# Seven half-width products for the queries of five heads, and an earlier first product for the gates, in a two-layer decoder on one Trainium2 core

## The chip, the cores and the metric

The kernel runs on one core of a Trainium2 chip, as one launch. The metric is the device time of that launch in microseconds; the median of several executions counts. Before the change it is 971.77 us (three runs, 971.26 to 971.91). One further execution was recorded by the hardware profiler.

## What is computed

A decoder trunk of two layers over 528 positions (16 learned meta tokens and 512 tokens) of width 1024, all in float32. The first layer is gated linear attention, the second differential attention with 8 heads. The change is in the second. Cut to it, the reference says:

```python
proj = xn @ w_in                                  # 528x1024 @ 1024x8192
q, k, v, z = jnp.split(proj, 4, axis=-1)          # each 8 heads x 256
s = q_m @ k_m.T * 128 ** -0.5 + bias              # two score maps a head, m = 0, 1
p = softmax(where(dist >= 0, s, -inf))
a = p[0] - lam * p[1]
o = head_rms(a @ v) * gnorm * (1 - lambda_init)
h = h + (silu(z) * o) @ w_out
```

Then a final RMSNorm is applied and the meta positions are dropped.

## The kernel before, in words

**Numbers in two parts.** Matrix products run on TensorE in a float32 form of less precision. Each operand x is therefore split: ScalarE writes a rounded part `hi`, VectorE the rest `lo = x - hi` (`split`, L270 to L280), and a product is three: hi hi, hi lo, lo hi. A weight tile of 128 x 1024 so costs one operation of 1024 elements on each of the two engines before it can be used. In the profile the parts are named wh and wl, a11h and a11l, q (both), k (both) and so on.

**Two ways to project.** The plain way (`project`, L414 to L425) makes a block of 128 outputs for 512 tokens from 8 pieces of the inner dimension, three products each: 24 matmuls of 512 columns a block; a head's 256 outputs are two blocks, 48 matmuls. The other way (`Unit`, L436 to L536) cuts weights and inputs in 2 x 2 blocks and makes the product from seven products of half size in place of eight (Winograd's form of Strassen's scheme), each of 12 matmuls over 256 columns (264 with the meta tokens): 84 matmuls. For it VectorE first forms sums of weight blocks (`want_unit`, L356 to L385: four additions of 512 elements), and weights are split as a11, a12 and a22 (512 elements each) and two pairs of sums (1024 each). The inputs' sums are made once for all heads. The products p1 to p7 go into PSUM banks bx, by and bv; ScalarE copies what the bank bx holds after p1, p6 and p7 (`partial`, L450, three copies u1, u2, u3 of a sum that grows), and VectorE adds the pieces (`add`, L472). The first product of a unit, p1 (`first`, L455), can be issued by the unit before it, so that its copy is done in time; such a unit is called early. A unit looks up what follows it in the queue when it starts (`following`, L86).

**The order of work.** TensorE's instructions stand in the order in which the code issues them. A `Weaver` (L74) holds a queue of generators, each a projection that yields its estimated time as it goes; `fill(us)` runs the head of the queue for so many estimated us. Between the steps of a head's attention the main loop (L1849 to L1905) calls `fill`, so that projections for the next head stand between the attention steps of this one: A is `scores` (L1679), B `turn` (L1703), C `values` (L1716), E `rows` (L1735), for four blocks of 128 queries each. The order in a steady head is: output projection of two earlier heads (`q_diff_out2`, L1766, half of the columns a head), gates z, values v, keys k, queries q for the next head. z, v and k are units of seven products; q is plain (`q_diff_q`, L1662). In head 6 the order is keys, queries, values, gates. The first `fill` of a head, 3.0 us, stands ahead of its first scores (L1888).

The instructions of the other engines are ordered by a scheduler with priorities; `soon`, `urgent` and `at_once` (L254 to L265) raise them by 40, 100 and 160. Each engine takes its instructions in that order, so one that waits holds up those behind it.

**Weights.** `Weights` (L154) loads 1 MB a unit through SP's queue into one of two buffers `raw`, and makes the split parts when a buffer of their kind is free: two of the pairs, one each of sum, a11, a12, a22. `done` (L199) gives a part's buffer back when its product has been issued. The values of a head are also turned by DMA: they leave through ScalarE's queue, and come back by transposes on SP's queue (L598, L600), which stand there ahead of the gates' weights.

**Scores.** For each block and each of the two maps, TensorE fills a bank ps, VectorE adds the bias T and takes the extreme (L1692), ScalarE takes the exponential and its sum (L1694). Then VectorE forms lam times the ratio of the two sums (L1697, L1698) and combines the maps (L1699).

Of the kernel before, what the change touches and what calls it, by code (L numbers as in the profile page):

```python
# [73 lines left out]
class Weaver:  # L74


    def __init__(self):
        self.queue, self.late, self.left, self.stop = deque(), [], 0.0, None
        self.away, self.behind, self.gated = [], [], ()
# [130 lines left out]
def trunk(ctx, tc, x, meta, g_norm, gla_w_in, gla_w_gate_up, gla_b_gate, gla_gnorm, gla_w_out,  # L210
# [53 lines left out]
    def at_once(fn):  # L264
        return urgent(fn, 160)  # L265
# [170 lines left out]
    class Unit:  # L436
# [17 lines left out]

        def first(self):  # L455
            a11 = self.u[0]
            w = ws.use(a11)
            self.bx = pb_tile(self.tags[0])
            yield from product(self.bx, w, self.X["b11"])
            ws.done(a11)  # L460
            self.p1 = self.partial()

        def run(self):
# [40 lines left out]
            def p7():  # L504
                yield from product(self.bx, ws.use(s43)[1], X["t3"], False)
                self.u3 = self.partial()
                add(1, 1, self.bv, self.u3, -1)
# [994 lines left out]
    up[0] = ep  # L1502
# [159 lines left out]
    def q_diff_q(hd, s):  # L1662
        want_diff(256 * hd)

        def gen():
            for i in range(2):
                bank = pb_tile("bx" if hd else ("bv", "by")[i])
                yield from project(ws.take(), real2, None, NR, [by_halves(bank)])
                assert not hd or heads[hd - 1].scored
                if i == 0:  # L1670
                    s.q = [T(ep, [P, 2, NR], F32R, f"q{j}", bufs=1) for j in range(2)]
                urgent(split)(*[t[:, i, :] for t in s.q], bank, scale=-float(P) ** -0.5)
        return W.add(gen(), 10.3)

    def diff_steps(hd, s, ys):
# [3 lines left out]
        def scores(b):  # L1679
# [4 lines left out]
            r.p = []  # L1684
            ko = L - nk
            for m in range(2):
# [8 lines left out]
                r.p.append(p[:, :nk])  # L1695
# [70 lines left out]
    def q_diff_out2(hd, yp, halves):  # L1766
# [5 lines left out]
        def gen():  # L1772
            for i in halves:
                banks = [pb_tile(tag) for tag in ("bx", "by", "bv", "bx")]
                cs = slice(512 * i, 512 * (i + 1))
                for j, h in enumerate(parts[i]):
                    w = ws.use(h)
                    for b in range(4):
                        for k in range(2):
                            y = [t[:, k, b * P:(b + 1) * P] for t in yp[j]]  # L1780
                            mm3(banks[b], y, w[k], j == k == 0, j == k == 1)
                        if j:
                            W.mark = dve.tensor_tensor(hacc[:, b, cs], hacc[:, b, cs], banks[b], op=ALU.add)
                        yield 1.4
                    ws.done(h)
# [62 lines left out]
    for hd in range(D_HEADS):  # L1848
# [39 lines left out]
        W.fill(3.0)  # L1888
# [80 lines left out]
```

## Time and profile before

| what | value |
|---|---|
| median of three runs | 971.77 us |
| the profiled execution's own time | 970.65 us |
| its span, first to last instruction | 968.9 us |
| TensorE busy (matmul) | 957.2 us, 99% |
| VectorE busy | 778.6 us, 80% |
| ScalarE busy | 626.8 us, 65% |
| GpSimd busy | 44.9 us, 5% |
| moved by DMA | 104.94 MB, mean 108 GB/s |

The page gives one execution. PE is TensorE's matmuls, PEld its weight loads, which overlap the matmuls; DVE is VectorE, ACT ScalarE, POOL GpSimd, SP the queue that issues loads. A row names the line, the engine, the operation, what it writes and reads (out<-in), the shape and the count; behind the bar stand busy time and mean ns, and then the idle time of the engine just before these instructions, with what ended it. Matmuls are pipelined, so that their durations overlap: the distance from one start to the next is what counts. A row in the slices gives, for a stretch of time, the busy time of PE, PEld, DVE, ACT and POOL with the number of instructions, then the granted clock of TensorE, the share in which the DMA engines were busy, and GB/s. A steady head of the second layer lasts some 63 us.

### The profile page before, as it was taken

To read this page: it belongs to the slowest core of one execution; us is meant where nothing else is said; L and a number is where in the kernel's file an instruction comes from. 1 tells how busy PE (TensorE), PEld (TensorE's weight loads), DVE (VectorE), ACT (ScalarE), POOL (GpSimd) and SP (SyncE) were. 2 spreads that over 40 slices of the span, in tenths; PEclk is the share of its full clock that TensorE was granted. 3 is DMA by queue.
4 is the path that set the end of the run, shared out by engine and by line. 5 is a ranking of instruction groups with operands and counts; after the bars stand their busy time and mean duration, and the time that the engine had idled before them with its cause. 6 is when DMAs were issued, how large, how long until landed. Compare 5 with 4: busy or idle time off the path is not lost.

```text
span 968.9 us, 18048 instructions
## 1 busy us (share of the span) xinstructions
PE 957.2 (99%) x6993; PEld 906.9 (94%) x6993; DVE 778.6 (80%) x1586; ACT 626.8 (65%) x1304; POOL 44.9 (5%) x68
## 2 busy tenths in 40 slices
PE   9999999999999999999999999999999999999997
PEld 8999999999999999998899998998999989989996
DVE  7989885886888787668997987968869769687785
ACT  7776755577647567656757776575675756755583
POOL 1000000000000000000001001000000000000001
PEclk9999999999999999999999999999999999999999
DMA  7322223635363236124355525243342341722212
GB/s 197 88 85 59 82 79 122 147 103 128 116 162 91 85 117 158 53 101 152 99 130 138 143 73 133 75 139 98 99 138 88 118 119 44 182 70 84 89 64 87
DMA packets 128522, 104.94 MB, mean 108 GB/s; under 512 B 51102, under 2 KB 112830, under 8 KB 128433
## 3 DMA queue, kind: packets, MB, share of 16 engines
q1 hardware_dynamic: 123104, 93.80, 35.1%
q10 hardware_dynamic: 5328, 9.95, 2.8%
q8 instruction: 56, 0.92, 0.4%
q14 instruction: 34, 0.27, 0.1%
HBM read 83.64 MB, written 11.80 MB: 99 GB/s over the span
## 4 chain that ended last, share of the span: by engine, by line
PE 88%; ACT 1%; DVE 1%; issue 1%; POOLq 0%; DVEq 0%
PE bx L431 19%; PE bv L431 12%; PE by L431 10%; PE bx L421 10%; PE ps L400 9%; PE bx L972 5%; PE bx L400 3%; PE bv L972 2%; PE by L972 2%; PE ps L1214 2%; PE by L400 2%; PE bv L400 2%; PE ps L1807 1%; PE bx L1807 1%; PE bv L421 1%; PE by L421 1%
## 5 line engine op out<-in xcount | busy, mean ns | idle before, releaser
L277 DVE TENSOR_TENSOR wl<-raw,wh 128x1024 fp32r<-128x1024 f32 x98 | 119.4, 1221 | 23.0 <-ACT wh L276 18.9
L276 ACT ACTIVATE wh<-raw 128x1024 fp32r<-128x1024 f32 x98 | 103.1, 1054 | 48.3 <-PE by L972 22.9
L431 PE MATMUL bv<-x,wh 128*128 128x264 f32 (+1 forms) x656 | 98.6, 287 | 0.0
L431 PE MATMUL bx<-x,wh 128*128 128x264 f32 (+1 forms) x640 | 95.6, 286 | 0.0
L431 PEld LDWEIGHTS bv<-x,wh 128*128 128x128 f32 x656 | 86.8, 189 | 0.6 <-DVE z L479 0.2
L431 PEld LDWEIGHTS bx<-x,wh 128*128 128x128 f32 x640 | 84.6, 188 | 0.7 <-ACT u L452 0.2
L452 ACT ACTIVATE u<-bx 128x264 f32<-128x264 f32 (+1 forms) x120 | 45.3, 379 | 35.5 <-PE bx L431 33.1
L1694 ACT ACTIVATE p<-p,st 128x528 f32<-128x528 f32 (+3 forms) x64 | 36.5, 570 | 41.7 <-DVE st L1692 41.4
L421 PE MATMUL bx<-x,wh 128*128 128x512 f32 (+1 forms) x256 | 62.4, 385 | 0.0
L277 DVE TENSOR_TENSOR wl<-sum,wh 128x1024 fp32r<-128x1024 f32 x41 | 50.1, 1221 | 10.6 <-ACT wh L276 10.5
L431 PE MATMUL bx<-x,wl 128*128 128x264 f32 (+1 forms) x320 | 54.1, 284 | 0.0
L431 PE MATMUL bv<-x,wl 128*128 128x264 f32 (+1 forms) x328 | 53.8, 284 | 0.1
L421 PEld LDWEIGHTS bx<-x,wh 128*128 128x128 f32 x256 | 44.4, 188 | 7.8
L276 ACT ACTIVATE wh<-sum 128x1024 fp32r<-128x1024 f32 x41 | 43.1, 1051 | 9.7 <-PE by L972 3.9
L431 PE MATMUL by<-x,a12h 128*128 128x264 f32 (+1 forms) x320 | 47.5, 286 | 0.1
L1730 POOL TENSOR_TENSOR st<-st,mhalf 128x1 f32<-128x1 f32 x32 | 25.5, 795 | 468.6 <-ACT on L1728 418.2
L431 PE MATMUL bx<-x,a11h 128*128 128x264 f32 (+1 forms) x320 | 46.6, 284 | 0.0
L431 PEld LDWEIGHTS bv<-x,wl 128*128 128x128 f32 x328 | 45.4, 188 | 0.3 <-issue 0.3
L431 PEld LDWEIGHTS bx<-x,wl 128*128 128x128 f32 x320 | 45.3, 188 | 0.3
L431 PEld LDWEIGHTS bx<-x,a11h 128*128 128x128 f32 x320 | 42.4, 188 | 0.6
L431 PEld LDWEIGHTS by<-x,a12h 128*128 128x128 f32 x320 | 42.1, 188 | 0.3 <-ACT t L1658 0.3
L276 ACT ACTIVATE a11h<-raw 128x512 fp32r<-128x512 f32 x41 | 25.7, 626 | 20.7 <-DMA raw<-in_diff_w_in_dram 7.9
(493 smaller groups left out, 2631.9 us busy)
## 6 DMA issues: line engine op xcount, KB each, us to landing
raw<-in_gla_w_in_dram SPq DMA_DIRECT2D x48, 512.0 KB, 4.5
raw<-in_diff_w_in_dram SPq DMA_DIRECT2D x42, 512.0 KB, 4.9
raw<-in_diff_w_in_dram SPq DMA_DIRECT2D x11, 1024.0 KB, 5.9
raw<-in_gla_w_out_dram SPq DMA_DIRECT2D x8, 1024.0 KB, 5.8
raw<-in_diff_w_out_dram SPq DMA_DIRECT2D x8, 1024.0 KB, 6.0
vd<-planes ACTq DMA_DIRECT2D x12, 268.0 KB, 5.8
vd<-keep ACTq DMA_DIRECT2D x12, 264.0 KB, 2.3
T<-bdr SPq DMA_DIRECT2D x8, 264.0 KB, 4.7
```

What stands on the lines that cost most here:

```text
L276: act.activation(hi, src, AF.Copy)
L277: dve.tensor_tensor(lo, src, hi.bitcast(F32), op=ALU.subtract)
L400: pe.matmul(ps, l, r, start=first and n == 0, stop=last and n == 2, **kw)
L421: pe.matmul(bank, a[:, k, :], b[k] if n0 is None else b[k][:, n0 + i * nn:n0 + (i + 1) * nn], start=n == 0 and ks[0] == 0, stop=n == len(t ...
L431: pe.matmul(bank[:, :x[q].shape[2]], w[p][:, k * P:(k + 1) * P], x[q][:, k, :], start=first and i == 0, stop=i == len(PASSES) - 1, skip_gr ...
L452: W.moved = act.activation(t, self.bx[:, :self.n], AF.Copy, scale=self.sc)
L972: pe.matmul(banks[i][:, :HT], h.t[p][:, k, mm * P:(mm + 1) * P], s.y[q][k][:, i * HT:(i + 1) * HT], start=n == 0, stop=n == len(PASSES) - 1)
L1214: pe.matmul(o, s.kd[:, i, kc], s.qs[:, i, t0:t0 + n], start=i == 0, stop=i == 1)
L1694: act.activation(p[:, :nk], p[:, :nk], AF.Exp, scale=-1.0, bias=st[:, m:m + 1], accum_out=st[:, 2 + m:3 + m])
L1730: pool.tensor_tensor(ms, ms, mhalf[:, :1], op=ALU.pow)
L1807: pe.matmul(ps[i], yp[hd][p][:, k, b * P:(b + 1) * P], wt[q][cs.start // 512][:, 2 * hd + k, cs.start % 512:(cs.stop - 1) % 512 + 1], star ...
```

## The change

The queries of heads 3 to 7 become units of seven products, with the scale in their additions and a split of the finished queries from SBUF. In the second layer a unit that is early and has no unit behind it, as these queries and the keys of heads 1 and 2 are, puts p7 into a bank of its own; VectorE adds it to u2 (`third`), in place of the growing sum in bx and ScalarE's copy. The output projection issues the first product of the gates behind it, ahead of the last of its own four groups; its additions to the residual get the highest priority. Of the two score maps, map 1 comes first. The first fill of a head is 4.0 us in place of 3.0.

```diff
@@ Weaver.__init__
-        self.away, self.behind, self.gated = [], [], ()
+        self.away, self.behind, self.gated, self.second = [], [], (), False
@@ class Unit
+        @at_once
+        def third(self, bank):
+            t = T(up[0], [P, HT], F32, "u", bufs=3)[:, :self.n]
+            if self.sc == 1.0:
+                dve.tensor_tensor(t, bank[:, :self.n], self.u2, op=ALU.add)
+            else:
+                dve.scalar_tensor_tensor(t, bank[:, :self.n], self.sc, self.u2, op0=ALU.mult, op1=ALU.add)
+            return t
+
@@ Unit.run
             def p7():
-                yield from product(self.bx, ws.use(s43)[1], X["t3"], False)
-                self.u3 = self.partial()
+                if W.second and early and not nxt:
+                    bank = pb_tile("bx")
+                    yield from product(bank, ws.use(s43)[1], X["t3"])
+                    self.u3 = self.third(bank)
+                else:
+                    yield from product(self.bx, ws.use(s43)[1], X["t3"], False)
+                    self.u3 = self.partial()
                 add(1, 1, self.bv, self.u3, -1)
@@ start of the second layer
-    up[0] = ep
+    up[0], W.second = ep, True
@@ q_diff_q
+        scale, qts = -float(P) ** -0.5, []
+
+        def tiles():
+            assert not hd or heads[hd - 1].scored
+            s.q = [T(ep, [P, 2, NR], F32R, f"q{j}", bufs=1) for j in range(2)]
+
+        if hd in (3, 4, 5, 6, 7):
+            def dst():
+                tiles()
+                qts.extend([tok_tile()[:, :NR], tok_tile()[:, :NR]])
+                return qts
+
+            @soon
+            def tail(i):
+                split(*[t[:, i, :] for t in s.q], qts[i])
+
+            return W.add(Unit(want_unit(d_w_in, 256 * hd), Xr, scale, dst, tail), 8.9)
         want_diff(256 * hd)
...
@@ scores
-            r.p = []
+            r.p = [None, None]
             ko = L - nk
-            for m in range(2):
+            for m in (1, 0):
...
-                r.p.append(p[:, :nk])
+                r.p[m] = p[:, :nk]
@@ q_diff_out2
         def gen():
+            nxt = W.following()
+            nxt = nxt if isinstance(nxt, Unit) else None
             for i in halves:
...
                         if j:
-                            W.mark = dve.tensor_tensor(hacc[:, b, cs], hacc[:, b, cs], banks[b], op=ALU.add)
+                            W.mark = at_once(dve.tensor_tensor)(hacc[:, b, cs], hacc[:, b, cs], banks[b], op=ALU.add)
                         yield 1.4
+                        if (i, j, b) == (halves[-1], 1, 2) and nxt:
+                            yield from nxt.first()
@@ main loop
-        W.fill(3.0)
+        W.fill(4.0)
```

On TensorE, at the end of head 4's queries (made during head 3) and the start of the output projection that head 4 issues, this stood before (bx is the second block of the plain query projection, then the output projection's first bank; ps the first scores, read from q and k):

```order
L421 MATMUL bx_11924<-x_1512_8554,wl_11870 128x512 x4
L421 MATMUL bx_11924<-x_1514_8556,wl_11870 128x512 x4
L400 MATMUL bx_11958<-wh_11971,y_1540_8780 128x512
L400 MATMUL bx_11958<-wl_11972,y_1540_8780 128x512
L400 MATMUL bx_11958<-wh_11971,y_1540_8780 128x512 x2
L400 MATMUL bx_11958<-wl_11972,y_1540_8780 128x512
L400 MATMUL bx_11958<-wh_11971,y_1540_8780 128x512
L400 MATMUL by_11959<-wh_11971,y_1540_8780 128x512
```

and this stands there now (by and bx take the products of a12 and a22, bv the last one; then again the output projection):

```order
L431 MATMUL by_12053<-x_1514_8556,a12l_11893 128x256 x4
L431 MATMUL bx_12067<-x_1544_8787,a22h_11990 128x256 x8
L431 MATMUL bx_12067<-x_1544_8787,a22l_11991 128x256 x4
L431 MATMUL bv_12013<-x_1514_8556,wh_11986 128x256
L431 MATMUL bv_12013<-x_1515_8557,wh_11986 128x256
...
L431 MATMUL bv_12013<-x_1514_8556,wl_11987 128x256 x4
L400 MATMUL bx_12098<-wh_12111,y_1540_8780 128x512
L400 MATMUL bx_12098<-wl_12112,y_1540_8780 128x512
```

The queries' 512-column products became products of 256 columns, and the output projection's groups follow at once as before, three of them ahead of the first scores in both.

On VectorE, at the same place, this stood before (a11l, sum, a12l and raw belong to head 5's gates, wl to the output projection, q to head 4's queries):

```order
L277 TENSOR_TENSOR a11l_11983<-raw_11968,a11h_11982 128x512
L277 TENSOR_TENSOR wl_11972<-raw_11962,wh_11971 128x1024
L280 SCALAR_TENSOR_TENSOR q_2134_11921<-bx_11878,q_2133_11920 128x512
L1740 TENSOR_TENSOR yt_11931<-ps_11928,z_10728 128x256
L366 TENSOR_TENSOR sum_11986<-raw_11968 128x512
...
L277 TENSOR_TENSOR a12l_12056<-raw_11968,a12h_12055 128x512
L366 TENSOR_TENSOR raw_11968<-raw_11968,sum_11986 128x4x128
L277 TENSOR_TENSOR wl_11976<-raw_11962,wh_11975 128x1024
L280 SCALAR_TENSOR_TENSOR q_2134_11921<-bx_11924,q_2133_11920 128x512
```

and now (u at L461 is the new third, t the additions of the queries' pieces):

```order
L461 SCALAR_TENSOR_TENSOR u_12046<-bx_12026,u_12011 128x256
...
L277 TENSOR_TENSOR a11l_12123<-raw_12108,a11h_12122 128x512
L490 SCALAR_TENSOR_TENSOR t_12050<-by_12053,u_11936 128x256
...
L486 SCALAR_TENSOR_TENSOR t_12051<-bx_12067,u_12046 128x256
L366 TENSOR_TENSOR sum_12126<-sum_12126,raw_12108 128x512
L366 TENSOR_TENSOR raw_12108<-raw_12108 128x4x128
L490 SCALAR_TENSOR_TENSOR t_12050<-bv_12013,u_12011 128x256
L277 TENSOR_TENSOR q_2165_12049<-t_12051,q_2164_12048 128x512
L277 TENSOR_TENSOR wl_12116<-raw_12102,wh_12115 128x1024
L277 TENSOR_TENSOR q_2165_12049<-t_12050,q_2164_12048 128x512
```

Four additions of the queries' pieces now stand among the work on the gates' weights, three of them behind a11l, and the query splits read their result from SBUF in place of PSUM.

5 lines of the change are left out of this document (2 added, 3 removed).

## The prediction

> **What bounds the kernel now.** I read the page first: span, busy shares, the chain that ended last.
>
> ```profile
> span 968.9 us, 18048 instructions
> PE 957.2 (99%) x6993; PEld 906.9 (94%) x6993; DVE 778.6 (80%) x1586; ACT 626.8 (65%) x1304; POOL 44.9 (5%) x68
> PE 88%; ACT 1%; DVE 1%; issue 1%; POOLq 0%; DVEq 0%
> ```
>
> TensorE holds 88% of the chain, no other engine over 1%. Next, a steady head and 5.25 us slices of it (columns: PE, PEld, DVE, ACT, POOL busy), and TensorE's groups there, idle time last.
>
> ```profile
> 669.48:732.51 63.03, 63.03 (x436) 58.70 (x435) 50.09 (x109) 41.14 (x92) 2.97 (x4) 1.00 0.35 106
> 660.10:665.35 5.25, 5.25 (x25) 4.25 (x24) 5.25 (x11) 3.62 (x7) 0.00 (x0) 1.00 0.00 0
> 681.10:686.35 5.25, 5.25 (x46) 5.25 (x45) 5.12 (x15) 2.84 (x7) 0.00 (x0) 1.00 0.66 201
> 702.10:707.35 5.25, 5.25 (x46) 5.24 (x45) 2.77 (x5) 4.76 (x8) 0.55 (x1) 1.00 0.06 21
> 717.85:723.10 5.25, 5.25 (x27) 4.29 (x26) 1.88 (x5) 3.76 (x9) 0.55 (x1) 1.00 0.71 215
> ...
> L421 PE MATMUL bx<-x,wh 128*128 128x512 f32 x32 | 8.4, 399 | 0.0
> L431 PE MATMUL bv<-x,wh 128*128 128x264 f32 (+1 forms) x48 | 7.4, 287 | 0.0
> ```
>
> Neither the query projection (L421) nor the seven products (L431) waits for anything: a head lasts 63.03 us because its matmuls do, at a granted clock of 1.00. What shortens TensorE's list shortens the head, as long as VectorE keeps up. VectorE runs full for whole slices (5.25 of 5.25 from 660.10) without a wait on TensorE; it is at ease in the key products (2.77) and the query projection (1.88). There the change puts its new work.
>
> **What a matmul costs** is read from the pieces of the chain, start and length, since their own durations overlap.
>
> ```profile
> 735.30 1.37 PE by L400 x6
> 742.47 1.43 PE by L431 x12
> 844.47 3.50 PE bx L421 x15
> ```
>
> 512 columns take 3.50/15 = 0.233 us, 256 columns 1.43/12 = 0.119.
>
> **The change, TensorE.** Queries of heads 3 to 7 were 2 blocks x 24 = 48 products of 512 columns: 48 x 0.233 = 11.20 us. Now they are 7 x 12 = 84 of 256: 84 x 0.119 = 10.01. That is 1.19 us a head, 5.95 for five. Nothing else on TensorE changes in number; the rest moves.
>
> On this pace there is a rule that speaks against the change. The Trainium skill (TensorE: Matmul & The Clock Gate, Back-to-back issue gap) says that pairs of weight load and matmul sustain about 81 ns at 128 columns and 131 ns at 512, so that columns cost little and each product much. An estimate on that line, 98 ns at 256, makes the queries 8.2 us against 6.3 and the five heads 9.7 us slower. This trace disagrees (0.119 and 0.233), and the trace decides.
>
> **The change, VectorE and ScalarE.** Durations of the same operations in the steady head, then starts that follow one another on VectorE.
>
> ```profile
> L277 DVE TENSOR_TENSOR wl<-raw,wh 128x1024 fp32r<-128x1024 f32 x7 | 8.6, 1222 | 1.0 <-ACT wh L276 1.0
> L277 DVE TENSOR_TENSOR a11l<-raw,a11h 128x512 fp32r<-128x512 f32 x3 | 2.1, 692 | 3.4 <-ACT a11h L276 3.4
> L280 DVE SCALAR_TENSOR_TENSOR q<-bx,q 128x512 fp32r<-128x512 f32 x2 | 1.4, 683 | 0.0
> ...
> L276 ACT ACTIVATE wh<-raw 128x1024 fp32r<-128x1024 f32 x7 | 7.4, 1054 | 1.1 <-PE bx L400 0.9 <-PE bv L431 0.2
> L276 ACT ACTIVATE a11h<-raw 128x512 fp32r<-128x512 f32 x3 | 1.9, 623 | 0.2 <-DMA raw<-in_diff_w_in_dram 0.2
> L279 ACT ACTIVATE q<-bx 128x512 fp32r<-128x512 f32 x2 | 1.2, 578 | 0.0
> L452 ACT ACTIVATE u<-bx 128x256 f32<-128x256 f32 x3 | 1.1, 382 | 2.2 <-PE bx L431 2.2
> ```
>
> ```profile
> 715.57 0.42 DVE L479 TENSOR_TENSOR t<-bv,u 128x264 f32<-128x264 f32 x1
> ...
> 716.02 1.23 DVE L277 TENSOR_TENSOR wl<-raw,wh 128x1024 fp32r<-128x1024 f32 x1
> 717.16 0.42 DVE L1740 TENSOR_TENSOR yt<-ps,z 128x256 f32<-128x256 f32 x1
> 717.49 0.68 DVE L277 TENSOR_TENSOR k<-t,k 128x512 fp32r<-128x512 f32 x1
> 718.09 0.42 DVE L277 TENSOR_TENSOR hT<-yt,hT 128x256 fp32r<-128x256 f32 x1
> ...
> 721.97 0.69 DVE L277 TENSOR_TENSOR a11l<-raw,a11h 128x512 fp32r<-128x512 f32 x1 [3.37 <-ACT a11h L276]
> ...
> 729.13 0.68 DVE L280 SCALAR_TENSOR_TENSOR q<-bx,q 128x512 fp32r<-128x512 f32 x1
> 729.73 1.28 DVE L576 TENSOR_TENSOR v<-planes,v 128x512 fp32r<-128x512 f32 x2
> ...
> 732.12 0.42 DVE L1692 CUSTOM_DVE_ANT_0 p<-ps,T 128x264 f32<-128x264 f32 x1
> ```
>
> Start to start, 1024 elements take 1.14 us (716.02 to 717.16), 512 take 0.60 (717.49 to 718.09), 256 from PSUM 0.33. A changed head loses two weight splits and two query splits: 2 x 1.14 + 2 x 0.60 = 3.48 us. It gains four weight additions and three single splits (7 x 0.60), two pair splits (2 x 1.14), four output additions and the new third (5 x 0.33), and two query splits from SBUF (2 x 0.60): 9.33. Net 5.85: VectorE goes from 50.1 of 63.0 us to 55.9 of 61.8, and its idle time from 12.9 to 5.9. ScalarE loses 2 x 1.05 + 2 x 0.58 = 3.3 and gains 3 x 0.62 + 2 x 1.05 + 2 x 0.38 + 2 x 0.58 (the splits from SBUF priced as those from PSUM) = 5.9: 43.8 of 61.8, no bound. All of this lies beside TensorE unless a product waits for it.
>
> **Where one could wait: the query's end.** From the third product's last matmul, TensorE has three groups of the output projection (3 x 1.37 = 4.1 us; the row at 735.30) and then the scores, whose map 0 needs the later query half about 1 us on (8 matmuls of 0.12): cover 5.1 us. Before, VectorE was done with the query at 729.73 and read its first score at 732.12, 2.4 us later. By the new order VectorE must do, behind that matmul (about 0.3 us until its result stands, from the 0.287 of one), the last addition, a query split, a weight split and the second query split: 0.3 + 0.33 + 0.60 + 1.14 + 0.60 = 3.0. Spare: 2.1 us.
>
> That holds if VectorE is not late when it gets there, and one thing makes it late: the gate's weights. Their first split (a11l) stands in front of those additions in the queue, and waits for ScalarE's a11h, which waits for the DMA, which on SP stands behind two transposes of the values. The rows of SP and ScalarE, in this head and a later one:
>
> ```profile
> 712.86 2.90 SPq L598 DMA_TRANSPOSE planes<-vd  x2
> ...
> 717.27 0.97 SPq L298 DMA_DIRECT2D raw<-in_diff_w_in_dram  x2
> ```
>
> ```profile
> 721.30 0.63 ACT L276 ACTIVATE a11h<-raw 128x512 fp32r<-128x512 f32 x1 [0.21 <-DMA raw<-in_diff_w_in_dram]
> ```
>
> ```profile
> 777.70 2.60 SPq L598 DMA_TRANSPOSE planes<-vd  x2
> ...
> 781.70 1.08 SPq L298 DMA_DIRECT2D raw<-in_diff_w_in_dram  x2
> ...
> 785.84 0.63 ACT L276 ACTIVATE a11h<-raw 128x512 fp32r<-128x512 f32 x1 [1.68 <-DMA raw<-in_diff_w_in_dram]
> ```
>
> The issue at 717.27 follows the split that frees the buffer (716.02 + 1.14), data are there 4.0 us later, the split 4.7. In the change that freeing split is the query's own second pair, still behind the keys' last addition (715.57), so a11l can start about 1.6 + 4.7 = 6.3 us after that addition; the query's last result stands 8.8 after it (six products of 1.43 and an attention transpose). Ahead of the last addition VectorE does a11l and three sums (4 x 0.60) and three operations of 0.33, 3.4 in all: it gets there at 9.7 instead of 8.8. So 0.9 of the 2.1 is used and 1.2 is left. The later head (781.70) had its weights issued 1.3 us later than 717.27 plus a period of 63.1: that would use it up. Bounds of this term: 0 in each head, and 1 us in each of five, 5 us; below nothing is excluded, since TensorE had no wait to lose there. I take 0.7 in all, near the low end: of the two heads shown only the later one uses the spare up.
>
> **Other edits, at no cost.** The gate's first product now stands inside the output projection, ahead of its last group: its bank is the one that the first group left, whose addition (0.60) has a 1.37 us group, two scores and another 1.37 to finish in; "additions first" holds that. If that cover went, up to 1 us a head, in the bound above. Scores in the order 1, 0 meet the half that is ready first. The first fill, 4.0 in place of 3.0, still takes three groups of 1.4. The third on VectorE costs 0.33 for ScalarE's 0.38. Five loads of 1 MB become ten of 0.5 MB on a queue that moves 35% of the time. In head 6 keys, queries, values and gates are now four units in a row with the last output weights behind them: the same 1.19 saved, VectorE closer to full, at most 1 us back.
>
> **Sum.** The profiled execution took 970.65 us (span 968.9 and 1.75 around it): 970.65 - 5.95 + 0.7 = 965.4. The median of the runs is 1.12 above it: 966.5, 0.54% faster. Within 0.2%, 1.9 us, a measurement cannot tell it from no change.
>
> **Rivals.**
> - *TensorE waits at the query's end.* For it: the late head above, and a VectorE with 5.9 us of idle time instead of 12.9. Against it: 1.2 us spare. Five heads waiting 0.9 us: 966.5 - 0.7 + 4.5 = 970.3. Chance 0.15, half of it outside 0.2%.
> - *VectorE becomes the bound; slower.* Its 12.9 us of idle time are waits for others (3.4 for a11h alone), and if these stay, a head lasts 55.9 plus them. It costs from 5.9 on and turns the sign at 63.0 - 55.9 = 7.1. At 8.2, two thirds of today's, a head takes 64.1, 1.1 more; five give 5.5: 977.3. For it: an in-order engine keeps such waits. Against it: full slices at 660.10 and 681.10 without a TensorE wait show that they vanish when a queue stands behind. Chance 0.11.
> - *Weight loads set the pace; slower.* Weight loads fill the slices of short products (5.25 of 5.25 from 681.10) and not that of long ones (4.29 from 717.85). If 84 loads in place of 48 raised the 0.119 above 11.20/84 = 0.133, the gain would be gone; at 0.150 it is 12.6 us, 1.4 more a head, 978.8. The rule of the Trainium skill quoted above would bring it about. The rows at 742.47 already hold these loads: chance 0.01.
> - *Head 6 and the last head crowd*: 2 us back, 968.5, chance 0.03. That the products don't change is excluded by the order.
>
> **How the numbers follow.** Forecast 0.70, rivals 0.15, 0.11, 0.01, 0.03. Faster: 0.70 + 0.07 + 0.03 = 0.80; same 0.08; slower 0.12. Low end: no wait at all and 1.30 us a head, were 256 columns to take 0.1178, 1% less: 971.77 - 6.5 = 965.3, and 0.5 for the measurement: 964.8. High end: the first rival and 0.5: 970.8. Left out are the two slower rivals.
>
> **What would show it.** Right: 420 more 256-column and 240 fewer 512-column products; a steady head of 61.8 to 62.0 us; TensorE idle 0.0 in it; VectorE 55 to 57 busy; the wait before a11l under 1.5 instead of 3.37. Wrong: a gap on TensorE ahead of the scores (L400 ps<-k,q) or of the third output group, with VectorE as releaser (first rival); gaps all over a head of 63 us or more (second); 256-column products over 0.13 us apart (third).

## The result: 0.3 to 0.45% slower, and where the time went

The changed kernel takes 976.13 us (median of 21 runs, 970.93 to 978.05) against 971.22 (21 runs, 970.61 to 971.93): a ratio of 1.0045, interval 1.0038 to 1.0051. A second series gave 973.38 (8 runs, 972.13 to 977.65), ratio 1.0034 (1.0021 to 1.0046). The forecast was 966.5. Single runs now differ by 7 us, before by 1.3; that is part of the finding.

The profiled execution took 976.1 us. Its page, to be read beside the first two lines of the prediction:

```profile
span 974.3 us, 18540 instructions
PE 955.8 (98%) x7173; PEld 913.8 (94%) x7173; DVE 806.6 (83%) x1648; ACT 636.5 (65%) x1327; POOL 46.7 (5%) x68
```

There are 180 more matmuls: 420 more of 256 columns at L431, 240 fewer of 512 at L421. The chain that ended last covers only 7% of the span here, so nothing is read from it. Three successive stages (a stage runs from a head's first scores to the next head's; columns as before) and three groups of the new query product, by start:

```profile
609.91:671.68 61.77, 61.77 (x471) 59.71 (x470) 52.82 (x115) 40.90 (x93) 3.23 (x4) 1.00 0.37 106
671.68:734.39 62.71, 62.58 (x471) 59.97 (x470) 55.95 (x124) 42.55 (x97) 3.21 (x4) 1.00 0.37 108
734.39:799.47 65.08, 62.98 (x472) 60.02 (x471) 55.84 (x122) 42.53 (x97) 3.12 (x4) 1.00 0.35 104
```

```profile
786.50 1.10 PE L431 MATMUL bx<-x,wh 128*128 128x256 f32 x8
...
787.92 1.10 PE L431 MATMUL bv<-x,wh 128*128 128x256 f32 x8
```

Twelve matmuls of 256 columns take 787.92 - 786.50 = 1.42 us, 0.118 each: the products are as cheap as forecast. The stage of head 2 takes the 61.8 us that were forecast, without a wait. The stage of head 4 takes 65.08, and there TensorE is busy for only 62.98.

To see all of it I laid the matmuls end to end, from the start times of all of them: 0.233 us for 512 columns, 0.118 for 256, between them by their columns, at least 0.109. What lies between starts beyond that is called waiting here (a halved clock counts in it; the small negative entries show the error of the method, some 0.2).

| stage | before, waiting | after, waiting |
|---|---|---|
| first layer, up to 470 us | 11.05 | 11.95 |
| up to the scores of head 0 | 1.38 | 1.43 |
| head 0 | 0.25 | **4.23** |
| heads 1 and 2 | -0.21 | -0.05 |
| head 3 | -0.11 | 0.82 |
| head 4 | -0.04 | **3.19** |
| head 5 | -0.08 | 0.34 |
| head 6 | 0.80 | **2.34** |
| head 7 | 0.12 | 0.43 |
| all matmuls, end to end | 947.53 | 941.25 |

The matmuls are 6.28 us shorter. The waiting is 11.5 us longer, 10.6 of it in the second layer, and 8.8 of that in three stages, those of heads 0, 4 and 6. TensorE's waits of before and after in the second layer (470 to 962 us of before, 470 to 967 of after; us in all, times, longest):

```profile
PE bx L421 <- DVE wl L277: 0.7, 1, 0.7
PE ps L400 <- DVE yt L1740: 0.2, 1, 0.2
```

```profile
PE ps L1767 <- ACT on L1761: 2.5, 1, 2.5
PE by L431 <- DVE t L486: 1.9, 1, 1.9
PE bx L421 <- DVE wl L277: 0.7, 1, 0.7
PE ps L400 <- DVE yt L1770: 0.6, 1, 0.6
PE ps L1753 <- DVE am L410: 0.6, 1, 0.6
PE ps L400 <- DVE aT L277: 0.4, 1, 0.4
...
```

**Head 0's stage.** No query by seven products is near. (The expectations below call the place "head 1", after the keys and queries projected there.) GpSimd, VectorE, ScalarE and TensorE around it, then the slices:

```profile
541.31 3.03 POOL L1760 TENSOR_TENSOR st<-st,mhalf 128x1 f32<-128x1 f32 x1 [7.84 <-ACT on L1758]
```

```profile
541.36 0.78 DVE L277 TENSOR_TENSOR k<-t,k 128x512 fp32r<-128x512 f32 x2
542.04 0.69 DVE L366 TENSOR_TENSOR raw<-raw 128x512 f32<-128x512 f32 x1
542.64 0.69 DVE L277 TENSOR_TENSOR a12l<-raw,a12h 128x512 fp32r<-128x512 f32 x1
543.25 0.69 DVE L366 TENSOR_TENSOR raw<-raw,sum 128x512 f32<-128x512 f32 x1
```

```profile
544.38 0.47 ACT L1761 ACTIVATE on<-ps,st 128x256 f32<-128x256 f32 x1 [3.15 <-POOL st L1760]
544.91 0.44 PE L1767 MATMUL ps<-ident,on 128*128 128x128 f32 x2 [2.45 <-ACT on L1761]
```

```profile
541.00:546.00 5.00, 2.55 (x13) 1.79 (x12) 3.73 (x10) 1.82 (x7) 3.03 (x1) 1.00 0.67 210
546.00:549.50 3.50, 3.50 (x12) 2.87 (x11) 3.48 (x6) 2.44 (x7) 0.55 (x1) 0.51 0.01 3
```

The power at L1760, which norms a block's rows, takes 3.03 us; undisturbed it takes 0.55. It ends 0.40 us behind the last of VectorE's additions from SBUF to SBUF (543.25 + 0.69 = 543.94; 541.31 + 3.03 = 544.34). ScalarE waits for it, TensorE for ScalarE, 2.45 us. Then the granted clock is 0.5 for 3.41 us, which costs some 1.4 more.

**Head 4's stage.** SP, VectorE, TensorE:

```profile
763.93 0.92 SPq L298 DMA_DIRECT2D raw<-in_diff_w_in_dram  x2
```

```profile
771.35 0.69 DVE L366 TENSOR_TENSOR sum<-raw 128x512 f32<-128x512 f32 x1 [2.45 <-DMA raw<-in_diff_w_in_dram]
...
774.00 0.69 DVE L366 TENSOR_TENSOR raw<-raw,sum 128x512 f32<-128x512 f32 x1
774.62 0.42 DVE L486 SCALAR_TENSOR_TENSOR t<-by,u 128x264 f32<-128x264 f32 x1
```

```profile
775.09 0.99 PE L431 MATMUL by<-x,a12h 128*128 128x264 f32 x6 [1.86 <-DVE t L486]
```

The weights of the next head's query are issued at 763.93 and reach VectorE at 771.35, 7.4 us later. VectorE stands still for 2.45 us at their first sum; three more sums and a split follow, and only behind them the addition (774.62) that empties bank by, for which the keys' next product waits.

A likely reason for the late load stands among the DMA packets. In the first 5 us behind the issue of the same load in head 3's stage (700.59), and then of this one (763.93), the trace has these queues (packets, MB, share of 16 engines):

```profile
q1 hardware_dynamic: 1143, 1.23, 76.6%
```

```profile
q1 hardware_dynamic: 1008, 1.02, 63.8%
q8 instruction: 1, 0.02, 3.6%
q14 instruction: 1, 0.01, 1.1%
```

The row q8 is a fetch of instructions, one packet of 16 KB that takes 2.9 us (3.6% of 16 engines for 5 us). The load's last packet ends 4.7 us after its issue in head 3's stage and 6.9 in head 4's. In all ten profiles of kernels with both the query units and the other edits, such a 16-KB packet begins 1.0 to 3.4 us after the issue of this load, and the load ends after 5.3 to 7.3 us. For the loads at the same place in the other heads, and for all of them in e1 and e16 below, none begins in that stretch, and the load ends after 4.6 to 5.1 us. No run moves the fetch by itself, so that it delays the load is argued from the timing, not shown.

**Head 6's stage** has three smaller waits (the last three rows of the waits above), for VectorE each time; keys, values, gates and the query of head 7 are all projected there.

### The profile page after: what moved, and what is told of

It reads as the page before. It is cut to its first block, busy times and chain, and to the rows that moved or that the text cites. A ratio compares the mean times of both kernels' runs of the same rounds, so it can differ in the third digit from the quotient of the medians.

```text
span 974.3 us, 18540 instructions
## 1 busy us (share of the span) xinstructions
PE 955.8 (98%) x7173; PEld 913.8 (94%) x7173; DVE 806.6 (83%) x1648; ACT 636.5 (65%) x1327; POOL 46.7 (5%) x68
## 5 line engine op out<-in xcount | busy, mean ns | idle before, releaser
L277 DVE TENSOR_TENSOR wl<-raw,wh 128x1024 fp32r<-128x1024 f32 x93 | 113.5, 1223 | 19.4 <-ACT wh L276 18.6
L431 PE MATMUL bv<-x,wh 128*128 128x264 f32 (+1 forms) x736 | 110.3, 287 | 0.1
L431 PE MATMUL bx<-x,wh 128*128 128x264 f32 (+1 forms) x720 | 106.2, 286 | 0.2 <-ACT u L452 0.2
L431 PEld LDWEIGHTS bv<-x,wh 128*128 128x128 f32 x736 | 97.0, 188 | 1.0 <-DVE z L488 0.3
L431 PEld LDWEIGHTS bx<-x,wh 128*128 128x128 f32 x720 | 94.6, 188 | 0.9 <-ACT u L452 0.4
L277 DVE TENSOR_TENSOR wl<-sum,wh 128x1024 fp32r<-128x1024 f32 x46 | 56.3, 1223 | 14.4 <-ACT wh L276 14.0
L431 PE MATMUL bv<-x,wl 128*128 128x264 f32 (+1 forms) x368 | 61.5, 285 | 0.1
L431 PE MATMUL bx<-x,wl 128*128 128x264 f32 (+1 forms) x360 | 59.3, 284 | 0.0
L431 PE MATMUL by<-x,a12h 128*128 128x264 f32 (+1 forms) x360 | 52.9, 286 | 2.0 <-DVE t L486 1.9
L431 PE MATMUL bx<-x,a11h 128*128 128x264 f32 (+1 forms) x360 | 53.2, 285 | 0.0
L431 PEld LDWEIGHTS bv<-x,wl 128*128 128x128 f32 x368 | 51.2, 189 | 0.4 <-issue 0.3
L431 PEld LDWEIGHTS bx<-x,wl 128*128 128x128 f32 x360 | 50.0, 188 | 0.3
L1760 POOL TENSOR_TENSOR st<-st,mhalf 128x1 f32<-128x1 f32 x32 | 27.2, 850 | 471.2 <-ACT on L1758 405.3
L276 ACT ACTIVATE a11h<-raw 128x512 fp32r<-128x512 f32 x46 | 28.9, 629 | 31.9 <-PE bx L431 11.5
L431 PEld LDWEIGHTS by<-x,a12h 128*128 128x128 f32 x360 | 46.9, 188 | 2.6 <-DVE t L486 2.2
L431 PEld LDWEIGHTS bx<-x,a11h 128*128 128x128 f32 x360 | 48.0, 188 | 0.7
L366 DVE TENSOR_TENSOR sum<-raw 128x512 f32<-128x512 f32 x46 | 31.7, 688 | 11.3 <-DMA raw<-in_gla_w_in_dram 5.2
L431 PE MATMUL by<-x,a22h 128*128 128x264 f32 (+1 forms) x280 | 40.5, 285 | 0.0
```

Of the source, the lines that this page charges most:

```text
L276: act.activation(hi, src, AF.Copy)
L277: dve.tensor_tensor(lo, src, hi.bitcast(F32), op=ALU.subtract)
L366: dve.tensor_tensor(o, a, b, op=ALU.add)
L431: pe.matmul(bank[:, :x[q].shape[2]], w[p][:, k * P:(k + 1) * P], x[q][:, k, :], start=first and i == 0, stop=i == len(PASSES) - 1, skip_gr ...
L1760: pool.tensor_tensor(ms, ms, mhalf[:, :1], op=ALU.pow)
```

## The experiments

Ratios are to the kernel before in the same series; in brackets the interval. What TensorE waited is worked out as in the table, from 470 us on (2.1 us before, 12.7 after).

**e1: the queries alone.** Before, with only the hunk on `q_diff_q` (heads 3 to 7 as units).

> The kernel before with the query units of heads 3 to 7 alone (growing sums, maps 0 then 1, first fill 3.0, the gate's first product at its old place). Theory one, the waits come with the queries' own work on VectorE (weight sums that wait for a late load ahead of other additions): no gain worth the name, 970 to 977 us, waits of 1 to 3 us on TensorE for additions in heads 3 to 7. Theory two, they come with the edits around the queries: the 6 us of products are gained, 965 to 967 us, and TensorE waits under 1 us in all.

970.48 us, 0.9997 (0.9988 to 1.0006). The matmuls fall by the same 6.28 us, but TensorE waits 7.7. Theory one's time came, but not its waits of 1 to 3 us for additions; the longest is 0.8, and three of the four longest are ahead of attention's products (ps):

```profile
PE ps L400 <- DVE yt L1756: 0.8, 1, 0.8
PE bx L431 <- ACT u L452: 0.7, 1, 0.7
PE ps L1739 <- DVE am L410: 0.5, 1, 0.5
PE ps L400 <- DVE q L277: 0.5, 1, 0.5
...
```

The query units give back by themselves what they save. Only a small part of it is at the query's end (the fourth row), where the first rival had it.

**e2: all but the queries.** The changed kernel with `if hd in ():`.

> The changed kernel with plain queries in all heads: all other edits alone. Theory one: as before the change, 970.5 to 972 us; if head 1's wait for the normalisation (2.5 us in the changed kernel, where head 1 has no query unit) comes back it is 974 to 975. Theory two: all of the 11 us of waits without the 6 us of gain, 980 to 983 us.

972.61 us, 1.0018 (1.0009 to 1.0027). The edits that I put at nothing cost 1.7 us. By the trace it is spread: 3.8 us of waiting for 2.1, a last matmul at 963.7 for 961.8. The time is just over theory one's 972 us, and far from theory two's. The two parts together (-0.3 and +1.7) do not make +4.4. What costs most in the changed kernel is in neither part's profile: in e1 the first fill is 3.0, the power in head 0 takes 0.57 us, and head 4's load ends after 4.8 us; in e2 there is no such load, and the power took 1.18.

**e3 and e4: without the power.** In the changed kernel (e3) and in the one before (e4), L1760 (L1730 before) becomes a copy on ScalarE, so the rows are not normed.

```diff
-            pool.tensor_tensor(ms, ms, mhalf[:, :1], op=ALU.pow)
+            act.activation(ms, ms, AF.Copy)
```

> The changed kernel without the reciprocal root of each row block on GpSimd: ScalarE copies the value instead, so rows are not normalised. Theory one A, GpSimd is held up while VectorE runs from SBUF to SBUF and this makes TensorE wait and lose its clock: head 1's wait of 2.6 us and 1.35 us of half clock go, 972 us and less scatter from run to run. Rival: the wait of that place is VectorE's or ScalarE's queue and stays, 975 to 977 us.

> The kernel before with the same copy in place of the reciprocal root (rows not normalised). Both theories: TensorE did not wait for it, so 970.5 to 971.5 us, no change of 0.1%. If it gains 1 us or more, part of what e3 shows is only the shorter chain.

e3: 971.8 us, 1.0007 (0.9998 to 1.0016); head 0's wait for the power is gone (one of 0.6 for VectorE's aT stands there), that of head 4 is as it was (1.9 us, the clock at 0.5 behind it). e4: 970.3 us, 0.9995 (0.9986 to 1.0004), no change. So the power costs the changed kernel 2.6 to 3.7 us and the one before nothing that can be measured.

**e5: a first fill of 3.0.** One number put back in the changed kernel.

> The changed kernel with one number put back: the first fill is 3.0 again instead of 4.0. Theory one (in head 1 GpSimd's power runs into an unbroken run of VectorE operations from SBUF to SBUF, and which operations meet there hangs on the packing of the whole head): one group more or less ahead of head 0 moves every later group, so the power in head 1 may or may not meet the run. If it does: 975 to 977 us, with a wait above 2 us ahead of ps<-ident,on in head 1 and a power of about 3 us. If not: 971 to 973 us, powers all under 2 us, and the wait of about 2 us ahead of by<-x,a12h in head 4 remains. Rival (the loss comes from VectorE's larger load everywhere): no difference, 975 to 977 us, whatever the power lasts.

972.25 us, 1.0010 (1.0001 to 1.0019). The power lasts 0.58 us, and head 0's wait is gone. Up to head 0's scores TensorE's matmuls are 29.46 us long instead of 30.53: in heads 0 and 1, which have no output projection to start with, a fill of 4.0 pulls 1.07 us more products ahead of the scores, and with that other VectorE work beside the power. All profiles agree: in the six with a second-layer fill of 4.0 and the power (the changed kernel, e2, e6, e9, e11, e13) that power took 1.18 to 3.04 us, in the seven with 3.0 (before, e1, e5, e12, e15, e16, e17) 0.57 or 0.58.

**e6: late sums.** In the changed kernel the weights of the queries of heads 3 to 7 are not touched before the keys' unit has begun, and their sums and first split stand behind the last addition issued by then.

```diff
@@ want_unit
+        def behind_add():
+            return tc.issue_after(W.mark.ins) if late else ExitStack()
...
+            with behind_add():
...
+        a11.hold = late
@@ Unit.run
+            if nxt and nxt.u[0].hold:
+                nxt.u[0].hold = False
+                ws.pump()
```

> The changed kernel; in heads 3 to 7 the sums and first split of the query's weights may only be issued behind the values' last addition, instead of ahead of it. Nothing else moves. Theory one (an in-order VectorE stood at sums whose weights had not landed, and the addition that frees a bank waited behind them): the 2.0 us ahead of by<-x,a12h in head 4 and its small neighbours go, the wait in head 1 (no query unit there) stays: 972.5 to 974.5 us. Rival (VectorE is too full, so the work put off is late for the query's own products): the wait returns ahead of the query's bx<-x,wh or bv<-x,wh, 975.5 us or more.

969.98 us, 0.9990 (0.9981 to 0.9999), with 7.6 us of waiting for 12.7. The same place on VectorE (its lines stand 11 further down):

```profile
765.20 0.43 DVE L497 SCALAR_TENSOR_TENSOR t<-by,u 128x264 f32<-128x264 f32 x1 [0.97 <-PE by L439]
768.63 0.69 DVE L280 TENSOR_TENSOR a22l<-raw,a22h 128x512 fp32r<-128x512 f32 x1 [3.00 <-ACT a22h L279]
...
771.18 0.68 DVE L280 TENSOR_TENSOR a11l<-raw,a11h 128x512 fp32r<-128x512 f32 x1
```

The weights are as late as before (ScalarE waits 2.84 us for them, and so VectorE 3.00 for ScalarE), but the addition is out of the way, and TensorE no longer waits ahead of by<-x,a12h. That is the second cause, shown. Not all waiting of that stage is gone: at 772.57 TensorE waits 0.5 us for an operation of VectorE (am) that stands behind the put-off split (771.18). The gain is more than the 2 to 4 us expected, and the profile says why: head 0's program is the same, but this time the power took 1.18 us:

```profile
540.30 1.18 POOL L1771 TENSOR_TENSOR st<-st,mhalf 128x1 f32<-128x1 f32 x1 [7.65 <-ACT on L1769]
```

So the median mixes both causes. What the late sums are worth alone shows beside the profiled execution of e9, the changed kernel with a power of 1.18 us too: 972.15 us there, 970.42 here. These 1.7 us come from one execution each; the wait that went is 1.9.

**e7: late sums and no power.** The power becomes `Ln` and `Exp` with scale -0.5 on ScalarE.

> As the last one, and GpSimd's power to -1/2 in each row block of the second layer's heads is replaced by a logarithm and an exponential (scale -0.5) on ScalarE; all is computed. Theory one (both local stoppages account for the loss): neither wait is left, the clock stays at 1.00, and of the forecast gain most is there: 967.5 to 969.5 us, faster than both kernels. Rival (VectorE is the bound, waits show up elsewhere): 971 to 973 us. If ScalarE has to load a table for the logarithm, about 1.3 us twice for each of 32 blocks on ScalarE's path: above 975 us.

1029.62 us, 1.0602 (1.0588 to 1.0617). ScalarE loads a table at each change, 64 times 1283 ns, 82 us. The experiment tells nothing of the waits.

**e9: the changed kernel again.**

> The changed kernel, unedited, beside the two that follow and on their chip, since the runs of it so far were on others. The program of head 1 is the same in the changed kernel and in the one with late sums, and the powers there lasted 3.03 and 1.18 us. Theory one (whether a power gets in between two VectorE operations is decided by hundredths of a microsecond, anew in each execution): the scatter stays as wide as it was, above 5 us, median 974 to 977 us. Rival (something of the place or the day made the changed kernel slow): a median under 973 us and a scatter like that of the others, 4 us.

973.38 us, 1.0034 (1.0021 to 1.0046), 5.5 us from end to end; the median is below what was expected. In its profile the power took 1.18 us and TensorE waited 0.7 for it; head 4's wait was there, with no halved clock. So head 0's hold is a matter of chance, execution by execution: with one and the same program there it was 3.03 us (the changed kernel), 3.04 (e11), 3.03 (e13) and 1.18 (e2, e6, e9). A mean granted clock of 0.996 or less was seen in 11 of the 29 runs of the changed kernel and in none of 121 of the one before; but head 0 is not its only source, since e3, without the power, has it in 2 of 11 runs, and e5, where the profile's half clock stands behind head 4's wait, in 5 of 11.

**e11 and e13: fewer queries.** Late sums, with head 6's query (e11) or head 7's (e13) as before the change.

> The kernel with late sums, with head 6's query as it was before the change (48 products of 512 columns), heads 3, 4, 5 and 7 by seven products. Theory one (four units in a row in head 6 load VectorE, and TensorE waits 2.4 us there against 0.4 before, more than the 1.19 us it saves): those waits fall under 1 us, 0.5 to 1 us faster than with late sums alone, 969 to 969.5 us. Rival (the waits in head 6 belong to the other edits): they stay, and the time is 1.2 us longer, 971 us or more.

> The kernel with late sums, with head 7's query as it was before the change; it is projected in the stage of head 6 (the run without head 6's query had it in the stage of head 5, where nothing waits, and lost 1.2 us of matmul time without touching the waits). Theory one (in the stage of head 6 four units stand in a row, and TensorE waits 2.4 us there against 0.4 before the change and in the kernel with the other edits alone): those waits fall under 1 us, worth 1.5 to 2 us, against 1.2 us more of matmuls: 0.3 to 0.8 us faster than late sums with all five, 0.9975 to 0.9985 of the kernel before. Rival (they belong to the order of the scores or the hoisted gate product): they stay, 1.2 us slower, 1.000 or more.

e11: 972.04 us, 1.0009 (0.9999 to 1.0019): by the letter the rival's outcome, but I had picked the wrong query; that of head 6 is projected in the stage of head 5. e13: 970.91 us, 0.9999 (0.9990 to 1.0008). The waiting in head 6's stage fell from 2.75 us to 1.11, for 1.25 us more of matmuls. So the crowd is there, but the exchange is worth little, and the median of e13, which has the hold of head 0 in its profile, did not improve.

**e12 and e15: fill 3.0 with late sums**, with all five queries and without head 7's.

> The kernel with late sums, with the first fill at 3.0 instead of 4.0. Theory one (the fill moves one group of products across head 0, which by itself costs nothing, and shifts what the power of head 1 meets): powers in head 1 under 1 us, no wait there, 969 to 970 us. Rival (the larger fill is a gain by itself): slower than with late sums alone by over 1 us.

> As the one without head 7's query, with the first fill at 3.0. Theory one (head 1's power can then not meet the run of six operations): no execution with a granted clock of 0.5 in the middle, scatter 3 us or less, 0.997 to 0.9985 of the kernel before. Rival (fill 3.0 only moves the place): as without it or slower.

971.29 us, 1.0002 (0.9993 to 1.0011), and 970.67, 0.9997 (0.9988 to 1.0006). My edit changed four fills of the first layer as well, and the waiting up to 470 us rose from 11.3 to 13.3 us there. From 470 us on it was 6.9 and 4.8 us, the least so far with query units. Both times are above theory one's, and e15's runs scatter by 3.8 us.

**e16: late sums, four queries, none of the other edits.**

> The kernel before with the seven products for the queries of heads 3 to 6 and late sums, without any of the other edits. Matmul time falls by 5.0 us (four heads at 1.25). Theory one (late weights and head 6 took the gain of the queries alone, which came out at 0.9997): most waits go, except those ahead of ps<-k,q at the end of the query, about 0.5 us in two or three heads: 0.996 to 0.998. Rival (the waits at the query's end, which the other edits take away, are the ones that count): 0.999 or more.

970.38 us, 0.9996 (0.9987 to 1.0005), the rival's side. TensorE waits 6.2 us, among them 0.60 ahead of ps<-k,q and 0.93 ahead of bx<-x,wh around head 3, which the next run, with the other edits, does not have.

**e17: late sums, four queries, the other edits with a first fill of 3.0** in the second layer alone.

> Late sums, head 7's query as before the change, and only the second layer's first fill at 3.0; the two kernels with fill 3.0 so far had four fills of the first layer changed with it, and lost 2.3 us there (TensorE's excess over its matmuls up to 470 us was 13.3 us against 11.0). Theory one (what is left of the loss is head 1's power, which fill 3.0 keeps out of VectorE's run): no clock of 0.5 in the middle, 968 to 969 us, 0.997 to 0.9985 of the kernel before, faster than both kernels. Rival (the power meets another run, or the waits in heads 4 and 6 are other than they were): 0.999 or more.

968.86 us (967.68 to 969.89), 0.9981 (0.9972 to 0.9990), as theory one expected: faster than both kernels, by 2.0 us than the one before and, by the medians, by 4.5 to 7.3 than the changed one. TensorE waits 5.1 us from 470 us on; the longest single wait in the profile is 0.5, for VectorE's am. Head 4's load is late here too (6.6 us), and no product of the keys waits for it.

**e8, e10, e14, e18: the power by itself.** Small kernels with powers of 128x1 on GpSimd beside various work.

> Not the reference's computation: eight powers of 128x1 one after the other on GpSimd, seven times, each time beside other work: nothing; VectorE additions of 128x512 from SBUF to SBUF without a break; the same with one operand in PSUM; two from SBUF and one of 264 from PSUM in turn; VectorE copies of 128x512 from SBUF; additions of 128x1024; ScalarE copies of 128x512. Theory one (VectorE's SBUF-to-SBUF additions hold GpSimd up): powers of about 0.55 us in the first, third and last part, and in the second and sixth at least one power of over 2 us, at worst to the end of the run of additions (9 to 10 us); in the fourth, powers end in the PSUM operations, 1 to 2 us each. Rival (the long powers in the kernel come from something else, a DMA or a clock): 0.55 to 0.7 us in all seven.

> Not the reference's computation: five powers of 128x1 on GpSimd, seven times, beside nothing; beside 12 VectorE additions of 128x512 from SBUF to SBUF that write three tiles in turn, so that each may begin before the one before has ended (as in the kernel, 0.60 us from start to start); beside 7 such additions of 128x1024; 12 of 128x512 with one operand in PSUM; runs of two, then of five, 128x512 from SBUF with one 128x264 from PSUM between the runs; and 12 that write one tile, as in the run before this one (0.72 us from start to start, powers 0.65 us). Theory one (a power gets in only where VectorE's SBUF operations leave a gap, and a run that overlaps leaves none): in the second and third part the first power lasts to the end of the run, 6 to 8 us; in the fourth 0.55; beside runs of two and five it ends in the PSUM operation, up to 1.2 and 3 us. Rival (a power waits for one operation at most, and the 3 us came from elsewhere): no power above 1.5 us in any part.

> Not the reference's computation: VectorE's six operations of head 1 (256, 512, 16, 4x128, 512, 4x128 columns, all from SBUF to SBUF, two of them with fp32r results) 14 times, and each time one power of 128x1 on GpSimd that starts 0.05 us later than the time before, by a ScalarE copy of 24 to 648 columns ahead of it. Theory one (it hangs on hundredths of a microsecond whether the power gets in at the 16-column operation or only behind the whole run): some powers of 0.6 to 1.3 us, and at least one of over 2 us that ends 0.4 us behind the last operation. Rival (in the kernel something else holds it, which this piece lacks): none above 1.5 us, as in the two runs of powers alone.

> Not the reference's computation: as the piece with 14 phases, where the powers began 0.41 to 0.95 us behind the 512-column operation's start and none took over 1.10 us; in head 1 the long one began 0.05 us ahead of it. One more addition of 512 columns stands in front, so that powers begin from about 0.2 us ahead of that operation to 0.35 us behind it, in 15 steps of 0.04 us; and the 15 once more while a load of 0.5 MB runs. Theory one (the phase decides): at least one power over 2 us at a start near 0.05 us ahead of the 512-column operation. Rival (something else of the kernel is needed): none above 1.5 us in the first 15; if it is the load, some in the second 15.

Eight powers in a row in e8: alone, beside VectorE additions of 512 elements from SBUF, beside such with one operand in PSUM, beside additions of 1024 from SBUF, beside ScalarE copies:

```profile
1.23 5.29 POOL L276 TENSOR_TENSOR st<-st,mhalf 128x1 f32<-128x1 f32 x8
8.61 6.09 POOL L276 TENSOR_TENSOR st<-st,mhalf 128x1 f32<-128x1 f32 x8
20.20 4.93 POOL L276 TENSOR_TENSOR st<-st,mhalf 128x1 f32<-128x1 f32 x8
...
52.16 10.28 POOL L276 TENSOR_TENSOR st<-st,mhalf 128x1 f32<-128x1 f32 x8
64.36 4.93 POOL L276 TENSOR_TENSOR st<-st,mhalf 128x1 f32<-128x1 f32 x8
```

The two parts not shown took 5.39 us (additions from SBUF and one operation on PSUM in turn) and 7.00 (copies from SBUF). Only operands that all come from SBUF hold it, and the longest single power was 1.46 us, where theory one expected over 2. e10, with additions that overlap, had none longer (1.46), and e14, with head 0's own run of operations, none over 1.10. e18 moved the start past that of the 512-element operation; two neighbours:

```profile
36.46 0.55 POOL L264 TENSOR_TENSOR st<-st,mhalf 128x1 f32<-128x1 f32 x1 [4.01 <-ACT st L254]
36.51 0.69 DVE L240 TENSOR_TENSOR r<-a,b 128x512 fp32r<-128x512 f32 x1
...
41.28 1.12 POOL L264 TENSOR_TENSOR st<-st,mhalf 128x1 f32<-128x1 f32 x1 [4.03 <-ACT st L254]
41.31 0.68 DVE L240 TENSOR_TENSOR r<-a,b 128x512 fp32r<-128x512 f32 x1
```

A power that starts 0.05 us ahead of the operation goes through in 0.55; one that starts 0.03 ahead ends 0.41 us behind the operation's end (41.31 + 0.68 = 41.99; 42.40). In 30 powers, with a load running or not, none was held by a second operation. So theory one holds for one operation and falls beyond it: VectorE's additions hold a power until the one that it met has ended. What makes it miss four in head 0 is not settled. That a power can miss more than one operation did not come with the change: the kernel before has a power in head 1's stage that met two operations and ended 0.41 us behind the second (571.81 + 0.68 = 572.49; 572.90):

```profile
570.63 2.27 POOL L1730 TENSOR_TENSOR st<-st,mhalf 128x1 f32<-128x1 f32 x1 [24.76 <-ACT on L1728]
```

```profile
570.67 1.22 DVE L277 TENSOR_TENSOR wl<-sum,wh 128x1024 fp32r<-128x1024 f32 x1
571.81 0.68 DVE L366 TENSOR_TENSOR raw<-raw,sum 128x512 f32<-128x512 f32 x1
```

TensorE came to those rows only at 575.18 and did not wait. A hold costs time where no other products cover it, and the larger fill put one at such a place.

## Why the prediction was wrong, point by point

- **TensorE's list**, -5.95 us: right (-6.28). The rivals on the weight loads' pace and on products that don't change are out.
- **VectorE's and ScalarE's load**, 55.9 and 43.8 us a head: right (55.95 and 42.5). The second rival came out near in time (977.3), but not over whole heads as it had it: VectorE has 7 to 9 us idle in these stages, and the first of them lasts 61.77. One of its kept waits did reach TensorE, the 2.45 us of head 4. (Its 8.2 is 0.64 of the 12.9, not two thirds.)
- **The waits, 0.7 us: the step that failed.** They are 10.6 us more than before in the profiled execution. I had looked for them in one place, the query's end, behind the gates' weights. There the cover held: the wait before a11l, forecast under 1.5 us, is 0.9 at most. The mechanism was the one that I described, a queue in order that stops at weights that have not landed with an urgent addition behind, but for the query's own weights, a stage earlier, among the values' and keys' products. "Five loads of 1 MB become ten of 0.5 MB on a queue that moves 35% of the time" looked at the queue's share and not at who stands behind the one load that is late. e6 shows that order to be the cause; what makes the load late, 6.9 us against 4.7, is argued above.
- **"Other edits, at no cost"**: they cost 1.7 us (e2). "The first fill, 4.0 in place of 3.0, still takes three groups of 1.4" holds from head 2 on; heads 0 and 1 start with products of 0.33 us a group, and there it takes 1.07 us more (e5).
- **GpSimd** was left out, since it is busy for 5%. Its 0.55 us stand on TensorE's path, and what VectorE runs beside them decides what they become: 2.5 us of waiting and a halved clock in some executions (e3, e5). The hold and the clock's price had no term.
- **Head 6 and the last head**, a rival with a chance of 0.03: right in place, and about in size (1.5 us more waiting in head 6, 0.3 in head 7, against 2).
- **The range** took in the first rival's five times 0.9 us. Each cause by itself would have fitted: head 0's stop is worth 2.3 to 3.7 us by e3 and e5, head 4's late load about 2 by e6 beside e9, head 6's waits 1.5. They came together, and I had no case in which they do.

What is left open: why the power can miss four operations, whether the instruction fetch is what delays head 4's load, what of e2's 1.7 us belongs to which edit, and whether five queries without these waits reach the forecast: e17 has four of them and is 2.4 us away, with 5.1 us of waiting left where the kernel before has 2.1.

## What to carry to other kernels

Follow every load that a change adds to the operation that stands behind its first reader in an in-order queue, not only the loads near the place you think critical: an urgent operation behind a late load waits as long as the load is late. A small operation on an idle engine counts by its place on the path, not by its share of the span; look what the neighbouring engine will be doing beside it. And when a scatter of 1 us becomes one of 7, look for a race between engines before you look for a cost.

## What the runs showed of the hardware that I had not expected

- **VectorE holds GpSimd.** A power of 0.55 us ends 0.40 us behind the end of the VectorE addition that it met, if both of the addition's inputs are in SBUF; with one in PSUM, or beside ScalarE, it does not notice (4.93 us for eight, each 0.55 and a gap). The Trainium skill (SBUF — State Buffer, Who interferes with whom) says that a VectorE instruction with two SBUF inputs contends with a GpSimd instruction that reads SBUF, and calls the ports that they share an exclusive lock. The small kernels agree, operation by operation; that a power misses two (2.27 us, before) or four (3.03 us) is not in that rule.
- **The clock halves after less than I thought.** It was 0.5 for 3.41 us after a wait of 2.45 us (a slice with TensorE busy for 2.55 of 5.00), and after the 1.9 us of head 4 in e3 and e5, but not after the same 1.9 us in the changed kernel and in e9. The Trainium skill (TensorE: Matmul & The Clock Gate, What's actually happening) has the half clock after an idle window of about 3.4 us that runs freely. The runs agree with a window that runs freely: where a profile has several half clocks, their starts lie whole multiples of 3.413 us apart (423.25 us, 124.0 windows, in the changed kernel, e11 and e13; 194.56, 57.0, in e3 and e5). The idle time that was enough here is shorter.
- **A load can be late beside an instruction fetch.** The load of 1 MB followed above ended 4.6 to 5.1 us after its issue, and 5.3 to 7.3 us in head 4 of the ten profiles in which a 16-KB instruction packet began 1.0 to 3.4 us after the issue; no run tests it apart.
- **ScalarE's tables.** Logarithm and exponential in turn cost 1283 ns for each of 64 table loads (e7).
